# Gate products of a product-key expert layer: one 128-column matmul per token and half in place of two of 64 columns

## The chip, the cores and the metric

The kernel runs on one core of a Trainium2 chip. The metric is device time in microseconds (us), from the first to the last instruction of the program plus what lies around them, and a lower time is better. A core has five engines with queues of their own: TensorE (PE in the profile; its weight loads are listed apart as PEld), VectorE (DVE), ScalarE (ACT), GpSimd (POOL) and SyncE (SP), which here only starts transfers. Matmul results go to PSUM, eight banks of 512 fp32 values per partition; DVE and ACT read them from there.

## The reference, cut to what matters

The program is two transformer blocks on 256 tokens of width 1024. The change touches one layer of the first block, the expert layer. For each token and each of 8 heads it takes the 16 best of 128 x 128 experts, found as sums of two lists of sub-scores, and a softmax over those 16 gives gates:

```python
    cand_i = (top_i[..., 0, :, None] * PEER_NKEYS + top_i[..., 1, None, :])...
    fin_s, fin_pos = lax.top_k(cand_s, PEER_TOPK)
    expert_idx = jnp.take_along_axis(cand_i, fin_pos, axis=-1)
    gates = jax.nn.softmax(fin_s, axis=-1)
...
        u_sel = jnp.take(u, ec, axis=0)
        act = jax.nn.gelu(jnp.einsum('chkd,cd->chk', u_sel, hc), approximate=False) * gc
        v_sel = jnp.take(v, ec, axis=0)
        return jnp.einsum('chk,chkd->cd', act, v_sel)
```

An expert is a pair (i, j) of indices below 128. So each token has 128 selections (8 heads times 16), each with an i, a j and a gate.

## The kernel before, in words

The kernel gathers nothing. It computes the activations of all 16384 experts for all tokens, multiplies them by a dense gate matrix that is zero where an expert was not selected, and multiplies the result by all of v. Expert (i, j) lies at unit i, partition j.

The U stage has 128 units, one for each i. A unit is one weight tile of 128x1024 fp32 (512 KB). SP loads it (`w`, line 322), ACT rounds it to `wh` (line 288), POOL subtracts to get the rest `wl` (line 292), and PE runs 24 matmuls of 256 columns from line 370: 16 with `wh` (against the high and the low part of the activations) and 8 with `wl`. ACT then writes GELU of the bank into `Ah` (line 1234). `Ah[0]` holds units 0 to 63, `Ah[1]` units 64 to 127. There are three buffers each of `w`, `wh` and `wl`. The V stage has 128 units too: for each, ACT and DVE split one unit of `Ah` into `zz` (lines 241 and 238), and PE runs 24 matmuls into four PSUM banks that accumulate over the whole stage (lines 1341, 1343 and 1345).

Between the two stand the gates. For a token, the gate matrix of one half (64 values of i) is a product over its 128 selections: a one-hot of j (128 selections x 128 j) as the stationary operand, and a one-hot of i times the gate (128 selections x 64 i) as the moving one. The gate is kept as two fp16 parts, `sel[0]` and `sel[1]`, so that there are two products per token, which add up in PSUM. `gbatch` does 8 tokens: DVE builds the j one-hot `ohJ` (line 1251), the i one-hot `ohI` (line 1253) and its two products with the gate parts `gI` (line 1256), all in fp16 and all with the token as the innermost index; PE runs 16 matmuls (line 1264) into one bank; and DVE multiplies the bank into `Ah` in place (line 1268). A half has 32 batches, in two lanes that alternate (`gate_lane`). Half 0 runs beside units 64 to 127 of the U stage, half 1 beside the first units of the V stage; unit 64 of the V stage needs all of half 1.

The order on each engine comes from a planner in the kernel, `Sched`. Work is written as generators of `Op`s with an engine, a cost in ns and dependencies. The planner keeps a clock per engine, emits the op that can start first by these costs, and places PE's main work with `sch.pe`, which first lets everything be emitted that could start before it. An op for PE is held back by `SLACK` (450 ns). A higher cost on DVE therefore moves the ops behind it, and the gate matmuls that depend on them, to a later place among PE's units. Each engine then runs its queue strictly in that order.

Of the kernel before, what the change touches and what calls it, by code (L numbers as in the profile page):

```python
# [24 lines left out]
AF = mybir.ActivationFunctionType  # L25
OP = mybir.AluOpType
# [4 lines left out]
S = 256  # L31
# [169 lines left out]
def tile_kernel(ctx, tc, A, out):  # L201
    nc = tc.nc
    V, ACT, POOL, PE, SP = nc.vector, nc.scalar, nc.gpsimd, nc.tensor, nc.sync
# [684 lines left out]
    for i, (key, j) in enumerate(order2):  # L888
# [7 lines left out]
        g = post_gate(key, j) if key in ("gs", "gc") else posts[key](j)  # L896
# [146 lines left out]
    acc2 = cpool.tile([128, S], F32, name="accp")  # L1043
    RpD = cpool.tile([128, 384], F32, name="RpD")
# [15 lines left out]
    hT = cpool.tile([128, 2, S], F32, name="hT")  # L1060
# [157 lines left out]
    sm_ = epool.tile([128, 16 * S], HF, tag="e0b", name="selT")  # L1218
    for i, key in enumerate(("i", "j", 0, 1)):
        sel[key] = sm_[:, i * S:(i + 1) * S]  # L1220
    iotax = sm_[:, 5 * S:9 * S].rearrange("p (n t) -> p n t", t=8)

    def prep_iota():
        yield Op("dve", c_dve(1024), lambda: V.tensor_copy(iotax, iota[:, :, None].to_broadcast([128, 128, 8])),
                 ev="iotax")

    sch.spawn(prep_iota(), prio=900.0)

    Ah = [None, None]
# [11 lines left out]
    ohF = [None]  # L1241

    def gbatch(hh, t0, pool):
        q = (t0 // 8) % 2
        ohJ = ohF[0][:, q * 1024:(q + 1) * 1024].rearrange("p (n t) -> p n t", t=8)
        ohI = ohF[0][:, 2048:2560].rearrange("p (n t) -> p n t", t=8)
        gb = ohF[0][:, 2560:4096] if q == 0 else sm_[:, 9 * S:15 * S]
        gI = [gb[:, i * 512:(i + 1) * 512].rearrange("p (n t) -> p n t", t=8) for i in range(2)]
        sl = slice(t0, t0 + 8)
        bc = lambda v, n: v[:, None, sl].to_broadcast([128, n, 8])  # L1250
        yield Op("dve", c_dve(1024, 0, True), lambda: V.tensor_tensor(
            ohJ, iotax, bc(sel["j"], 128), op=OP.is_equal), deps=[("sel", t0 // 128), "iotax", ("Gp", hh, t0 - 16)])
# [5 lines left out]
        b = [None]

        def f():  # L1260
            b[0] = pool()
            for t in range(8):
                for i in range(2):
# [566 lines left out]
    for n in range(4):  # L1830
        p = mmb()
# [7 lines left out]
    for s in range(2):  # L1839
        p = mmb()  # L1840
# [270 lines left out]
```

## Time and profile before

| | |
|---|---|
| median of 3 runs | 1807.87 us (1806.69 to 1808.79) |
| the profiled execution | 1811.32 us, its span 1809.5 us |
| busy share of the span | PE 93%, DVE 68%, POOL 66%, ACT 44% |
| granted TensorE clock, mean | 0.954 |
| matmuls | 13460 |

The profile gives for each engine the time its instructions took; an instruction that waits for a shared resource after it has started counts as busy. The chain that ended last is followed back from the last instruction, at each step to what released it. A granted clock of 1 is 2.4 GHz, and half of it 1.2 GHz. A row that merges several instructions says how many there were behind an x.

### The profile page before, as it was taken

Reading aid. Unit: us, or ns where it says so; the run is one execution under the profiler, and the core shown is the slowest. Engines: PE = TensorE matmul, PEld = TensorE weight load, DVE = VectorE, ACT = ScalarE, POOL = GpSimd, SP = SyncE. Lnnn points to the kernel's source line nnn. Section 1 sums busy time; section 2 is a strip of 40 time slices with the busy share of each in tenths; the row PEclk is TensorE's granted clock in tenths of the full one; section 3 lists DMA queues with packets and bytes.
Section 4 is the critical chain, followed back from the end, with each engine's and each line's share of the span. In section 5 each row is a group of like instructions: output and inputs, shape, how many; then the busy total and the mean of one; then the engine's idle time right before and its main releaser. Section 6 shows DMA issues by size and latency. Waiting matters only on the chain.

```text
span 1809.5 us, 33154 instructions
## 1 busy us (share of the span) xinstructions
PE 1688.5 (93%) x13460; PEld 1666.1 (92%) x13460; DVE 1222.8 (68%) x1994; ACT 803.3 (44%) x1302; POOL 1185.9 (66%) x509
## 2 busy tenths in 40 slices
PE   8898989898996999999999999999999889979997
PEld 7898989898996999999999999999999878979997
DVE  7999966658998706776006777889787897474302
ACT  5533445555443442222443223444444545656533
POOL 5677865456685884444884556887688633768885
PEclk8999999999998998888999999999999999999999
DMA  6454644445453453222553334555455331545553
GB/s 200 151 175 146 192 163 141 129 129 165 148 182 115 150 179 115 94 94 94 171 180 117 115 117 129 186 180 161 152 186 181 120 102 65 165 139 176 185 187 117
DMA packets 75305, 266.73 MB, mean 147 GB/s; under 512 B 8720, under 2 KB 9232, under 8 KB 75152
## 3 DMA queue, kind: packets, MB, share of 16 engines
q1 hardware_dynamic: 73856, 262.77, 44.8%
q8 instruction: 105, 1.72, 0.4%
q10 hardware_dynamic: 1296, 1.85, 0.3%
q14 instruction: 48, 0.39, 0.1%
HBM read 262.48 MB, written 2.10 MB: 146 GB/s over the span
## 4 chain that ended last, share of the span: by engine, by line
PE 61%; DVE 33%; ACT 3%; issue 2%; DMA 1%; POOL 0%; SPq 0%; DVEq 0%; ACTq 0%; POOLq 0%
PE mmb L370 29%; PE msb L1343 7%; PE msb L1341 7%; PE msb L1345 7%; DVE msb L607 5%; PE msb L1264 4%; PE mmb L1264 4%; DVE zz L238 3%; DVE scr L1182 1%; DVE scy L662 1%; DVE scr L1143 1%; DVE scr L1140 1%; ACT wh L288 1%; DVE scr L1179 1%; DVE scr L1142 1%
## 5 line engine op out<-in xcount | busy, mean ns | idle before, releaser
L292 POOL TENSOR_TENSOR wl<-w,wh 128x1024 fp32r<-128x1024 f32 x473 | 1162.2, 2461 | 591.4 <-ACT wh L288 413.3
L288 ACT ACTIVATE wh<-w 128x1024 fp32r<-128x1024 f32 x491 | 518.4, 1059 | 587.9 <-PE msb L1343 260.1
L238 DVE TENSOR_TENSOR zz<-Ah,zz 128x256 fp32r<-128x256 f32 x128 | 216.4, 1693 | 140.0 <-ACT zz L241 140.0
L370 PE MATMUL mmb<-hA,wh 128*128 128x256 f32 x1024 | 263.8, 293 | 1.2 <-ACT wh L288 1.2
L370 PE MATMUL mmb<-hB,wh 128*128 128x256 f32 x1024 | 262.1, 291 | 0.0
L1343 PE MATMUL msb<-zz,wh 128*128 128x256 f32 x1008 | 252.1, 287 | 7.8 <-DVE zz L238 7.7
L1341 PE MATMUL msb<-zz,wh 128*128 128x256 f32 x1008 | 253.2, 288 | 0.8 <-ACT zz L241 0.8
L370 PEld LDWEIGHTS mmb<-hA,wh 128*128 128x128 f32 x1024 | 206.6, 202 | 1.4 <-ACT wh L288 1.4
L370 PEld LDWEIGHTS mmb<-hB,wh 128*128 128x128 f32 x1024 | 205.6, 201 | 0.0
L1343 PEld LDWEIGHTS msb<-zz,wh 128*128 128x128 f32 x1008 | 197.1, 196 | 8.8 <-DVE zz L238 8.8
L1341 PEld LDWEIGHTS msb<-zz,wh 128*128 128x128 f32 x1008 | 197.2, 196 | 1.0 <-ACT zz L241 1.0
L370 PE MATMUL mmb<-hA,wl 128*128 128x256 f32 x1024 | 156.3, 299 | 0.4 <-POOL wl L292 0.4
L1345 PE MATMUL msb<-zz,wl 128*128 128x256 f32 x1008 | 145.0, 287 | 0.0
L370 PEld LDWEIGHTS mmb<-hA,wl 128*128 128x128 f32 x1024 | 142.1, 205 | 0.6 <-POOL wl L292 0.6
L370 PE MATMUL mmb<-hN,wh 128*128 128x256 f32 x896 | 120.4, 286 | 13.3 <-ACT hN L241 5.5
L1345 PEld LDWEIGHTS msb<-zz,wl 128*128 128x128 f32 x1008 | 132.3, 195 | 0.0
L1264 PEld LDWEIGHTS <-ohF 128*128 128x128 f16 x1024 | 121.5, 146 | 11.2 <-DVE ohF L1256 6.0
L370 PEld LDWEIGHTS mmb<-hN,wh 128*128 128x128 f32 x896 | 113.2, 195 | 15.3 <-ACT wh L288 6.7
L607 DVE SCALAR_TENSOR_TENSOR msb<-glu,vec,msb 128x256 f32<-128x256 f32 x232 | 113.1, 487 | 6.2
L1268 DVE SCALAR_TENSOR_TENSOR Ah<-msb,Ah 128x512 f32<-128x512 f32 x32 | 22.1, 692 | 101.3 <-PE msb L1264 101.3
L1234 ACT ACTIVATE Ah<-mmb 128x256 f32<-128x256 f32 x128 | 47.1, 368 | 84.0 <-PE mmb L370 84.0
L370 PE MATMUL mmb<-eu,wh 128*128 128x256 f32 x512 | 70.7, 287 | 6.4 <-DVE uHL L474 2.7
(465 smaller groups left out, 3268.1 us busy)
## 6 DMA issues: line engine op xcount, KB each, us to landing
w<-in_peer_u_dram SPq DMA_DIRECT2D x128, 512.0 KB, 3.5
w<-in_peer_v_dram SPq DMA_DIRECT2D x128, 512.0 KB, 3.5
w<-in_w_in_dram SPq DMA_DIRECT2D x81, 512.0 KB, 3.5
w<-in_w_up_dram SPq DMA_DIRECT2D x32, 512.0 KB, 3.5
w<-in_w_down_dram SPq DMA_DIRECT2D x32, 512.0 KB, 3.5
w<-in_w_peer_q_dram SPq DMA_DIRECT2D x16, 512.0 KB, 3.7
w<-in_w_v_dram SPq DMA_DIRECT2D x8, 512.0 KB, 3.5
w<-in_sc_w_out_dram SPq DMA_DIRECT2D x8, 512.0 KB, 3.6
```

The lines of the kernel that those rows point to most:

```text
L238: return lambda e="dve": ENG[e].tensor_tensor(o, a, b, op=op)
L288: yield Op("act", c_act(1024), lambda: ACT.activation(h, w, AF.Copy), deps=u["wdep"], ev=("H", u["i"]))
L292: lambda e: ENG[e].tensor_tensor(l, w, h.bitcast(F32), op=OP.subtract), ev=("L", u["i"]))
L370: PE.matmul(p[:, :S], a, b, start=first and n == 0, stop=last and n == len(todo) - 1)
L607: lambda k=k: V.scalar_tensor_tensor(cc[:, j] if k == 30 else o(), glu[:, j, k:k + S], vcol("cf_w", j * 31 + k), o(), op0=OP.mult, op1=OP. ...
L662: lambda k=k: V.scalar_tensor_tensor(y, b[:, k:k + S], vcol("sc_w", j * 3 + k), y, op0=OP.mult, op1=OP.add),
L1234: yield Op("act", c_act(S), lambda: ACT.activation(Ah[n // 64][:, n % 64], p[:, :S], AF.Gelu), ev=("U", n))
L1264: PE.matmul(b[0][:, t * 64:(t + 1) * 64], ohJ[:, :, t], gI[i][:, :, t], start=i == 0, stop=i == 1)
L1268: yield Op("dve", c_dve(512), lambda: V.scalar_tensor_tensor(z, b[0].rearrange("p (t i) -> p i t", t=8), 1.0 / GS, z, op0=OP.mult, op1=OP. ...
L1341: PE.matmul(o, u["H"][:, d, :], opH, start=first and d % 2 == 0, stop=False, skip_group_check=True)
L1343: PE.matmul(o, u["H"][:, d, :], opL, start=False, stop=False, skip_group_check=True)
L1345: PE.matmul(o, u["L"][:, d, :], opH, start=False, stop=last, skip_group_check=True)
```

## The change

`gbatch` is rewritten. The j one-hot stays as it was, with its token innermost. The i one-hot is built in token order (`p t n`) from a contiguous row `iotan` of the numbers 0 to 127, which ACT copies once as fp16. One DVE instruction of 1024 elements multiplies it by both gate parts, which lie side by side in `sel["g"]`, into `gT` (token, part, i). A token then needs one matmul whose moving operand is 128 contiguous columns, 64 for each part, and eight tokens fill two banks in two ops of four matmuls. The parts no longer add up in the accumulation: ACT copies the low half of a bank into fp32 scratch, DVE adds it to the high half in the bank, and DVE multiplies that into `Ah`. The scratch is `hT`, `RpD` and `accp`, which are free there. The planner's costs of the three DVE ops are written as 1000, 900 and 1700 ns, a gate matmul is put at 85 ns in place of 30, and the last ops have events of their own. The pool of banks is as before: `msb` in half 0, `mmb` in half 1, four banks each.

```diff
+    sel["g"] = sm_[:, 2 * S:4 * S].rearrange("p (a s) -> p a s", a=2)
+    iotan = sm_[:, 12 * S:12 * S + 128]
+    G_J, G_I, G_T = 1000.0, 900.0, 1700.0
...
-        yield Op("dve", c_dve(1024, 0, True), lambda: V.tensor_tensor(
-            ohJ, iotax, bc(sel["j"], 128), op=OP.is_equal), deps=[("sel", t0 // 128), "iotax", ("Gp", hh, t0 - 16)])
-        yield Op("dve", c_dve(512, 0, True), lambda: V.tensor_tensor(
-            ohI, iotax[:, hh * 64:(hh + 1) * 64], bc(sel["i"], 64), op=OP.is_equal), deps=[("Gi", hh, t0 - 8)])
-        for i in range(2):
-            yield Op("dve", c_dve(512, 0, True), lambda i=i: V.tensor_tensor(
-                gI[i], ohI, bc(sel[i], 64), op=OP.mult), ev=("Gi", hh, t0) if i == 1 else None)
...
-                    PE.matmul(b[0][:, t * 64:(t + 1) * 64], ohJ[:, :, t], gI[i][:, :, t], start=i == 0, stop=i == 1)
...
-        yield Op("pe", 16 * 30.0, f, ev=("Gp", hh, t0))
-        z = Ah[hh][:, :, sl]
-        yield Op("dve", c_dve(512), lambda: V.scalar_tensor_tensor(
-            z, b[0].rearrange("p (t i) -> p i t", t=8), 1.0 / GS, z, op0=OP.mult, op1=OP.mult), ev=("Z", hh, t0))
+        yield Op("dve", G_J, lambda: V.tensor_tensor(
+            ohJ, iotax, sel["j"][:, None, sl].to_broadcast([128, 128, 8]), op=OP.is_equal),
+            deps=[("sel", t0 // 128), "iotax", ("Gp", hh, t0 - 16)])
+        yield Op("dve", G_I, lambda: V.tensor_tensor(
+            ohI, iotan[:, None, hh * 64:(hh + 1) * 64].to_broadcast([128, 8, 64]),
+            sel["i"][:, sl][:, :, None].to_broadcast([128, 8, 64]), op=OP.is_equal), deps=[("Gi", hh, t0 - 8)])
+        yield Op("dve", G_T, lambda: V.tensor_tensor(
+            gT, ohI[:, :, None].to_broadcast([128, 8, 2, 64]),
+            sel["g"][:, :, sl].rearrange("p a t -> p t a")[:, :, :, None].to_broadcast([128, 8, 2, 64]),
+            op=OP.mult), ev=("Gi", hh, t0))
...
+                    PE.matmul(banks[c][:, t * 128:(t + 1) * 128], ohJ[:, :, 4 * c + t], gT[:, 4 * c + t],
+                              start=True, stop=True, skip_group_check=True)
...
+            yield Op("pe", 4 * 85.0, f(c), chain=c == 0, ev=("Gp", hh, t0) if c else ("Gc", hh, t0))
...
+            yield Op("act", 380.0, lambda view=view, lc=lc: ACT.activation(lc, view(1), AF.Copy),
+                     deps=[("Gp", hh, t0) if c else ("Gc", hh, t0)], chain=False, ev=("Ga", hh, t0, c))
+            yield Op("dve", c_psum(256), lambda view=view, lc=lc: V.tensor_tensor(view(0), view(0), lc, op=OP.add),
+                     deps=[("Ga", hh, t0, c)], chain=False, ev=("Gs", hh, t0, c))
+            yield Op("dve", c_psum(256), lambda view=view, z=z: V.scalar_tensor_tensor(
+                z, view(0), 1.0 / GS, z, op0=OP.mult, op1=OP.mult), deps=[("Gs", hh, t0, c)], chain=False,
+                ev=("Z", hh, t0) if c else None)
```

Lines behind the change are shifted: the gate matmuls stand at line 1274 of the changed kernel (1264 before), the three DVE ops at 1255, 1259 and 1262, the copy at 1284, the sum at 1286 and the multiplication at 1288.

On PE the order before in half 0 is 32 gate matmuls (both lanes), then 48 matmuls of U units, and so on 16 times, with 776 U matmuls behind the last. The changed order settles into 8 gate matmuls, 40 U matmuls, 8 gate matmuls and 56 U matmuls. Its first gate matmul stands 24 U matmuls later than before (576 behind the last transpose of the selection, where it was 552), and its last one 32 U matmuls ahead of the end of the stage. In half 1 the order before has 16 gate matmuls on either side of 8 V matmuls, once in every two units, and ends at unit 32. The changed order has 8 gate matmuls about every two units, from the third unit on, and its last three batches (24 matmuls) stand together behind unit 63.

DVE's queue in half 0 of the kernel before, one pair of batches (`ohF` and `selT` hold the one-hots, `msb` is the bank):

```order
L1251 TENSOR_TENSOR ohF<-selT 128x1024 x2
L1253 TENSOR_TENSOR ohF<-selT 128x512
L1256 TENSOR_TENSOR ohF<-ohF,selT 128x512 x2
L1253 TENSOR_TENSOR ohF<-selT 128x512
L1256 TENSOR_TENSOR selT<-ohF,selT 128x512 x2
L1268 SCALAR_TENSOR_TENSOR Ah_5368<-msb,Ah_5368 128x64x8 x2
```

And DVE's queue at the same place of the changed kernel, one batch and a half:

```order
740 L1255 TENSOR_TENSOR ohF_7689<-selT_5367 128x1024
741 L1259 TENSOR_TENSOR ohF_7689<-selT_5367 128x512
742 L1286 TENSOR_TENSOR msb_7916<-msb_7916,hT_4607 128x64x4
743 L1262 TENSOR_TENSOR selT_5367<-ohF_7689,selT_5367 128x1024
744 L1288 SCALAR_TENSOR_TENSOR Ah0_5368<-msb_7916,Ah0_5368 128x64x4
745 L1286 TENSOR_TENSOR msb_7921<-msb_7921,hT_4607 128x64x4
746 L1288 SCALAR_TENSOR_TENSOR Ah0_5368<-msb_7921,Ah0_5368 128x64x4
```

Before, both lanes' one-hots stand ahead of the two ops that wait for PE. Now the sum of the other lane (which waits for PE and then ACT) stands ahead of the product `gT` on which the next gate matmuls depend, and a batch has seven DVE instructions in place of five.

DVE's queue in half 1 of the kernel before, where `zz` is the split of `Ah` for the V units:

```order
895 L1251 TENSOR_TENSOR ohF_7688<-selT_5367 128x1024
896 L1256 TENSOR_TENSOR ohF_7688<-ohF_7688,selT_5367 128x512
897 L238 TENSOR_TENSOR zz_10442<-Ah0_5368,zz_10442 128x256
898 L1256 TENSOR_TENSOR ohF_7688<-ohF_7688,selT_5367 128x512
899 L1253 TENSOR_TENSOR ohF_7688<-selT_5367 128x512
900 L1256 TENSOR_TENSOR selT_5367<-ohF_7688,selT_5367 128x512 x2
901 L1268 SCALAR_TENSOR_TENSOR Ah1_7687<-mmb_11056,Ah1_7687 128x64x8
```

And in half 1 of the changed kernel:

```order
983 L1286 TENSOR_TENSOR mmb_10672<-mmb_10672,RpD_4281 128x64x4
984 L1262 TENSOR_TENSOR ohF_7689<-ohF_7689,selT_5367 128x1024
985 L238 TENSOR_TENSOR zz_10347<-Ah0_5368,zz_10347 128x256
986 L1288 SCALAR_TENSOR_TENSOR Ah1_7688<-mmb_10672,Ah1_7688 128x64x4
987 L1286 TENSOR_TENSOR mmb_10677<-mmb_10677,accp_4280 128x64x4
988 L1288 SCALAR_TENSOR_TENSOR Ah1_7688<-mmb_10677,Ah1_7688 128x64x4
989 L1255 TENSOR_TENSOR ohF_7689<-selT_5367 128x1024
990 L238 TENSOR_TENSOR zz_10347<-Ah0_5368,zz_10347 128x256
991 L1286 TENSOR_TENSOR mmb_10756<-mmb_10756,hT_4607 128x64x4
992 L1259 TENSOR_TENSOR ohF_7689<-selT_5367 128x512
```

The `zz` splits, which the next V units wait for, now stand between the new sums, each of which waits for PE and ACT.

## Rows read from the trace of the kernel before

**Rows 1.** The page: busy time by engine, and its chain by line.
```profile
PE 1688.5 (93%) x13460; PEld 1666.1 (92%) x13460; DVE 1222.8 (68%) x1994; ACT 803.3 (44%) x1302; POOL 1185.9 (66%) x509
...
PE mmb L370 29%; PE msb L1343 7%; PE msb L1341 7%; PE msb L1345 7%; DVE msb L607 5%; PE msb L1264 4%; PE mmb L1264 4%; DVE zz L238 3%; DVE scr L1182 1%; DVE scy L662 1%; DVE scr L1143 1%; DVE scr L1140 1%; ACT wh L288 1%; DVE scr L1179 1%; DVE scr L1142 1%
```

**Rows 2.** The chain in half 0: start, duration (us), what.
```profile
616.55 68.29 PE mmb L370 x552
684.84 3.95 PE msb L1264 x32
688.79 7.23 PE mmb L370 x48
696.01 3.95 PE msb L1264 x32
```

**Rows 3.** The chain from the end of the U stage into half 1.
```profile
857.20 94.50 PE mmb L370 x776
...
952.00 0.42 ACT zz L241
...
966.78 0.21 PE msb L1341
...
970.56 0.12 PE msb L1341
...
972.48 1.97 PE mmb L1264 x16
```

**Rows 4.** Windows: length, busy PE, PEld, DVE, ACT, POOL, clock, DMA share, GB/s.
```profile
684.00:858.00 174.00, 168.71 (x1244) 166.91 (x1244) 129.33 (x152) 42.76 (x61) 78.95 (x31) 0.85 0.30 98
...
960.00:1113.00 153.00, 152.61 (x1241) 151.01 (x1240) 113.48 (x186) 43.27 (x61) 77.91 (x31) 0.98 0.35 114
```

**Rows 5.** Timeline of PE: five fp32 matmuls of 128 columns, and what follows.
```profile
443.05 0.77 PE L1129 MATMUL msb<-pqF 128*128 128x128 f32 x5 [0.43 <-DVE pqF L474]
443.66 0.33 PE L370 MATMUL mmb<-pe0a,wh 128*128 128x256 f32 x1
```

**Rows 6.** Instructions of line 1264: ns min/median/max, first and last start.
```profile
L1264 PE MATMUL mmb<-selT,ohF x256: 295/302/333, 964.1 to 1112.9; 128*128 128x64 f16 x128
```

**Rows 7.** DVE and ACT instructions by line, ns min/median/max, first and last start.
```profile
L1251 DVE TENSOR_TENSOR ohF<-selT x30: 678/682/686, 963.2 to 1104.8; 128x1024 f16<-128x1024 f16 x30
...
L238 DVE TENSOR_TENSOR zz<-Ah,zz x31: 411/416/482, 959.8 to 1105.8; 128x256 fp32r<-128x256 f32 x31
...
L1268 DVE SCALAR_TENSOR_TENSOR Ah<-mmb,Ah x31: 690/691/693, 962.6 to 1110.3; 128x512 f32<-128x512 f32 x31
...
L1179 DVE TENSOR_TENSOR scr<-scr,cst x8: 1216/2175/3446, 556.6 to 609.1; 128x1024 f32<-128x1024 f32 x8
...
L238 DVE TENSOR_TENSOR mmb<-mmb,R x44: 416/432/433, 22.9 to 1707.4; 128x256 f32<-128x256 f32 x44
...
L1234 ACT ACTIVATE Ah<-mmb x128: 361/365/387, 474.0 to 951.7; 128x256 f32<-128x256 f32 x128
```

**Rows 8.** POOL's `wl` without gates beside it, and DVE's `zz` beside POOL.
```profile
L292 POOL TENSOR_TENSOR wl<-w,wh x32: 2377/2400/2400, 859.1 to 949.1; 128x1024 fp32r<-128x1024 f32 x32
...
L292 POOL TENSOR_TENSOR wl<-w,wh x43: 2397/2405/2600, 1116.3 to 1237.3; 128x1024 fp32r<-128x1024 f32 x43
...
L238 DVE TENSOR_TENSOR zz<-Ah,zz x40: 2417/2428/2433, 1116.6 to 1228.9; 128x256 fp32r<-128x256 f32 x40
```

**Rows 9.** Timeline of DVE and of POOL, where both always have work.
```profile
564.57 2.18 DVE L1179 TENSOR_TENSOR scr<-scr,cst 128x1024 f32<-128x1024 f32 x1
566.79 3.25 DVE L1182 TENSOR_TENSOR scr<-scr 128x1024 f32<-128x1024 f32 x1
570.07 1.22 DVE L1185 TENSOR_REDUCE scr<-scr 128x64 f32<-128x1024 f32 x1
571.21 2.12 DVE L1179 TENSOR_TENSOR scr<-scr,cst 128x1024 f32<-128x1024 f32 x1
...
562.56 12.96 POOL L292 TENSOR_TENSOR wl<-w,wh 128x1024 fp32r<-128x1024 f32 x4 [0.24 <-ACT wh L288]
```

More of the change, by code (lines that the diff above doesn't have):

```diff
@@ L1220, in tile_kernel @@
         sel[key] = sm_[:, i * S:(i + 1) * S]
-    iotax = sm_[:, 5 * S:9 * S].rearrange("p (n t) -> p n t", t=8)
+    sel["g"] = sm_[:, 2 * S:4 * S].rearrange("p (a s) -> p a s", a=2)
+    iotax = sm_[:, 4 * S:8 * S].rearrange("p (n t) -> p n t", t=8)
+    iotan = sm_[:, 12 * S:12 * S + 128]
+    G_J, G_I, G_T = 1000.0, 900.0, 1700.0
     def prep_iota():
+        yield Op("act", c_act(128), lambda: ACT.activation(iotan, iota, AF.Copy))
         yield Op("dve", c_dve(1024), lambda: V.tensor_copy(iotax, iota[:, :, None].to_broadcast([128, 128, 8])),
@@ L1245, in gbatch @@
         ohJ = ohF[0][:, q * 1024:(q + 1) * 1024].rearrange("p (n t) -> p n t", t=8)
-        ohI = ohF[0][:, 2048:2560].rearrange("p (n t) -> p n t", t=8)
-        gb = ohF[0][:, 2560:4096] if q == 0 else sm_[:, 9 * S:15 * S]
-        gI = [gb[:, i * 512:(i + 1) * 512].rearrange("p (n t) -> p n t", t=8) for i in range(2)]
+        ohI = ohF[0][:, 2048:2560].rearrange("p (t n) -> p t n", t=8)
+        gT = ohF[0][:, 2560:3584] if q == 0 else sm_[:, 8 * S:12 * S]
+        gT = gT.rearrange("p (t a n) -> p t a n", t=8, a=2)
@@ L1249, in gbatch @@
         sl = slice(t0, t0 + 8)
-        bc = lambda v, n: v[:, None, sl].to_broadcast([128, n, 8])
-        yield Op("dve", c_dve(1024, 0, True), lambda: V.tensor_tensor(
-            ohJ, iotax, bc(sel["j"], 128), op=OP.is_equal), deps=[("sel", t0 // 128), "iotax", ("Gp", hh, t0 - 16)])
-        yield Op("dve", c_dve(512, 0, True), lambda: V.tensor_tensor(
-            ohI, iotax[:, hh * 64:(hh + 1) * 64], bc(sel["i"], 64), op=OP.is_equal), deps=[("Gi", hh, t0 - 8)])
-        for i in range(2):
-            yield Op("dve", c_dve(512, 0, True), lambda i=i: V.tensor_tensor(
-                gI[i], ohI, bc(sel[i], 64), op=OP.mult), ev=("Gi", hh, t0) if i == 1 else None)
@@ L1258, in gbatch @@
[L1258 to L1263, printed above, removed]
-                    PE.matmul(b[0][:, t * 64:(t + 1) * 64], ohJ[:, :, t], gI[i][:, :, t], start=i == 0, stop=i == 1)
-        yield Op("pe", 16 * 30.0, f, ev=("Gp", hh, t0))
-        z = Ah[hh][:, :, sl]
-        yield Op("dve", c_dve(512), lambda: V.scalar_tensor_tensor(
-            z, b[0].rearrange("p (t i) -> p i t", t=8), 1.0 / GS, z, op0=OP.mult, op1=OP.mult), ev=("Z", hh, t0))
+        yield Op("dve", G_J, lambda: V.tensor_tensor(
+            ohJ, iotax, sel["j"][:, None, sl].to_broadcast([128, 128, 8]), op=OP.is_equal),
+            deps=[("sel", t0 // 128), "iotax", ("Gp", hh, t0 - 16)])
@@ new lines, in gbatch, with f, g @@
+        lo = ((hT[:, 0], hT[:, 1]), (RpD[:, :S], acc2[:, :]))[q]
+        banks = [None, None]
+        def f(c):
+            def g():
+                banks[c] = pool()
+                for t in range(4):
+                    PE.matmul(banks[c][:, t * 128:(t + 1) * 128], ohJ[:, :, 4 * c + t], gT[:, 4 * c + t],
+                              start=True, stop=True, skip_group_check=True)
+            return g
+        for c in range(2):
+            yield Op("pe", 4 * 85.0, f(c), chain=c == 0, ev=("Gp", hh, t0) if c else ("Gc", hh, t0))
@@ new lines, in gbatch @@
+        for c in range(2):
+            view = lambda i, c=c: banks[c].rearrange("p (t a i) -> p a i t", t=4, a=2)[:, i]
+            lc = lo[c].rearrange("p (i t) -> p i t", t=4)
+            z = Ah[hh][:, :, t0 + 4 * c:t0 + 4 * c + 4]
+            yield Op("act", 380.0, lambda view=view, lc=lc: ACT.activation(lc, view(1), AF.Copy),
[5 more added lines that the diff above has]
+                ev=("Z", hh, t0) if c else None)
```

## The prediction

> **What bounds the kernel now.** I read the page first. PE is busy for 93% of the span, and of the chain that ended last most is matmuls; the gate matmuls of line 1264 have two entries of 4% each [rows 1]. So in most of the program PE sets the pace, and time taken from PE there is time taken from the end, unless another engine comes up to it.
>
> Next the chain in the two stretches that the change touches. I call A the time from 616.55, where half 0's stretch begins, to the first `zz` of the V stage at 952.00 [rows 2, 3]: 335.5 us. In A the chain is all PE: 552 U matmuls in 68.29 us, then in turn 32 gate matmuls in 3.95 us and 48 U matmuls in 7.23 us, and at the end 776 U matmuls in 94.50 us [rows 2, 3]. A U matmul takes 94.50/776 = 0.122 us at the end. Between gate blocks it takes 7.23/48 = 0.151 us. The windows say why: the granted clock is 0.85 in the gate stretch of half 0, and 0.98 in that of half 1 [rows 4]. After 32 gate matmuls in a row PE runs for some microseconds at the lower level of 1.2 GHz; one sees such a spell in half 1 too, after a wait, where matmuls start 0.21 us apart and later 0.12 us, while 16 gate matmuls in 1.97 us are not followed by one [rows 3]. So half 0 loses 7.23 - 48 x 0.122 = 1.4 us per pair of batches, over 15 gaps 21 us.
>
> B is the time from 952.00 to the start of V unit 64, which needs all of half 1. The last gate matmul starts at 1112.9 [rows 6], and 32 units follow at the pace of POOL's 43 starts, (1237.3 - 1116.3)/42 = 2.881 us [rows 8]. B is 160.9 + 92.2 = 253.1 us.
>
> Then who else is near its limit there. POOL needs 2.40 us per unit of 2.88 us [rows 8]. DVE's two-input instructions wait for POOL: `zz` takes 0.416 us where POOL is off and 2.428 us where POOL always runs [rows 7, 8], the difference being most of a POOL instruction. So POOL's `wl` and every DVE instruction that reads two operands from SBUF share something that one of them holds at a time; I call it the port. DVE instructions with an operand in PSUM don't wait: 690 to 693 ns, always [rows 7].
>
> **The change part by part.** *Gate matmuls, removed.* 1024 become 512. What does one of 128 columns cost? Before, one of 64 fp16 columns takes 3.95/32 = 0.123 us [rows 2]. Five fp32 matmuls of 128 columns take 443.66 - 443.05 = 0.61 us, 0.122 each [rows 5], and U's of 256 columns the same 0.122. The pace doesn't follow the columns up to 256; the stationary side, unchanged here, sets it. Lower bound for the new one 0.061, half of it (no row here is faster than 0.12, but the moving operand is contiguous now); upper bound 0.245 (twice the columns, twice the time). I take 0.122, the nearest row. That is 256 x 0.122 = 31.2 us per half in place of 63.
>
> The Trainium skill (TensorE: Matmul & The Clock Gate, section Back-to-back issue gap) gives about 81 ns for a sustained stream with 128 columns. The row shows 122 ns. By the page a half would have 20.7 us of them, 10 less; in the sum below PE's pace is not the bound, so that it would not move.
>
> *The slow clock, removed.* Blocks are of 8 now, half of those of 16 that left the clock at 0.98 [rows 4]. I count U matmuls at 0.122.
>
> *DVE's one-hots, changed.* The j one-hot stays at 0.682 us [rows 7]. The i one-hot (512 elements) and the product (1024) have an operand repeated along the innermost index. The trace has no fp16 row of that kind. Lower bound: they keep the pace of line 1251, 0.682 us per 1024 and 0.42 per 512. Upper bound: the fp32 instruction of line 1179, the same shape with the same kind of repeated operand, 1.216 us unhindered [rows 7]; with `zz`'s 0.416 for 256 the slope is 0.800/768 = 1.04 ns per element, and 512 cost 0.683. I take the upper bound, since line 1179 is the row with that operand. Port time per batch is then 0.682 + 0.683 + 1.216 = 2.58 us.
>
> The Trainium skill (VectorE: DVE Perf Modes, What auto-detection actually checks) says that two results per cycle need 16-bit tensors with a step of 1 or -1, in every tensor. A repeated operand has a step of 0. The page speaks against this change, and agrees with the row that I took. By the lower bound 0.79 us per batch would go, and the forecast below would be about 40 us lower.
>
> *ACT's copies, DVE's sums, added.* 128 copies at about 0.37 us (line 1234 [rows 7]) are 47 us of ACT, which is busy 43 of 174 and 43 of 153 us there [rows 4]; hidden, at most 0.37 us of delay for a `wh` behind each. On DVE four PSUM instructions of 256 elements, 0.43 us each (line 238 on the bank [rows 7]), take the place of one of 0.69: 1.72 us per batch. They need no port, and can run while POOL does. If that cover goes, 1.72 x 64 = 110 us in place of 44 lie open.
>
> *Now the sum of the port.* In A the gates lie beside 2048 - 576 = 1472 U matmuls, 61.3 units, and 30 of the 32 batches are built there (two lanes are filled ahead, as before). POOL 61.3 x 2.40 = 147.2; DVE 30 x 2.58 = 77.4; together 224.6 us. PE: 1472 x 0.122 + 31.2 = 210.5 (by 94.50/776 unrounded). So the port overtakes PE. In B: POOL 64 x 2.405 = 153.9, `zz` 64 x 0.416 = 26.6, gates 32 x 2.58 = 82.6, together 263.1; PE 64 x 2.881 + 31.2 = 215.6.
>
> Lower bound of the port: some of an instruction doesn't hold it. From 564.57 to 571.21 pass 6.64 us [rows 9], with two DVE port instructions of 1.22 and, since POOL has one running whenever DVE waits, two of POOL's 2.40. (6.64 - 4.80)/2 = 0.92: each DVE instruction hides 0.30. A batch then costs 1.69, `zz` 0.12, and the sums are 198 in A and 215.7 in B, at PE's pace or below. Against that, both queues are strict: when DVE's head is a sum that waits for PE, nobody uses the port. I take the full sums, as if the hidden 0.30 paid for these gaps.
>
> A becomes 576 x 68.29/552 = 71.3 ahead of the gates, plus 224.6: 295.9, **39.6 less**. B becomes 263.1, plus the tail: three batches stand together ahead of unit 64, and behind the last one only its own chain runs (8 matmuls 0.98, copy 0.37, four DVE steps 1.72, `zz` 0.40 and 0.42): 3.9 us. 267.0, **13.9 more**. In sum 25.7 us less: the profiled execution at 1811.3 - 25.7 = 1785.6, and the median, 3.45 lower, at 1782.
>
> **Rivals.** *PE keeps the pace.* The lower port sums hold, and DVE and POOL fit beside PE: A 71.3 + 210.5 (-53.7), B 215.7 + 3.9 (-33.5), together -87: 1721. For it: in half 1 before, 32 batches at 1.95 us (one of 0.68, three of 0.42), 32 `zz` and 32 of POOL are 153 us of port in a window of 153, and PE was busy throughout [rows 4], so a full port need not hurt. Against it: that PE had more of its own then. The keeping of DVE's faster pace leads near it, to about 1743.
>
> *Slower: DVE's queue in half 1 never hides POOL.* Each POOL instruction finds DVE at a port instruction, as `zz` does all along rows 8, and the PSUM steps run only when POOL is off. A batch with two units then costs 2.58 + 1.72 + 0.83 + 4.81 = 9.94 us, B 318 + 3.9 = 322 (+69), and with A's -39.6 the kernel is 29 slower: 1837. It decides from 9.03 us per batch on, (253.1 + 39.6 - 3.9)/32; the forecast has 8.22. For it: the product stands behind the other lane's sum, and `zz` between them, so that a wait for PE passes on to PE. Against: POOL starts behind ACT's `wh`, not behind DVE, so that some overlap is likely.
>
> *The products cost by the column*, 0.245 each: PE 242 in A, -22, B still by the port, +14: 1800. Against it are rows 5.
>
> **How the numbers follow.** Forecast 0.52, PE's pace 0.20, slower 0.21, columns 0.07. The forecast's own range is 1762 to 1806. For 8 in 10 I take half of either outer case: 1738 to 1820. A measurement here tells 0.2%, 3.6 us, from no change. Faster: 0.48 of the forecast, 0.19 and 0.05, in sum 0.72. Same: 0.08. Slower: 0.20.
>
> **What would show it.** Right: gate matmuls 0.12 us apart, a clock near 0.95 or above in half 0, the product near 1.2 us unhindered, POOL's `wl` at more than 2.5 us on average beside the gates, PE waiting there for `wl` and for the product, A near 296 and B near 267. Wrong: PE without gaps in both halves (then 1721), B above 290 with DVE busy throughout (then slower), gate matmuls at 0.2 us or more.

## The result, and the profile after

The changed kernel takes 1783.82 us (median), the kernel before 1808.33 us beside it: ratio 0.9862, 95% interval 0.9838 to 0.9885. One of the four executions after was slow (1920.76 us, with a granted clock of 0.742); it is in the median and not in the ratio. The forecast was 1782. The profiled execution after is 1783.02 us, with a span of 1781.2.

I cut both spans at the same places: up to the last transpose of the selection, from there to the first `zz` (A), from there to V unit 64 (B), and the rest. So measured, the span before is 615.9 + 336.1 + 253.2 + 604.3, and after 613.3 + 286.8 + 272.2 + 608.8. A lost 49.3 us (forecast 39.6), B gained 19.0 (forecast 13.9), the rest gained 4.5, and the unchanged start lost 2.5. Unchanged code alone moves by amounts like the last two: over the runs below the start varies from 608 to 616, and the rest from 599 to 609.

First the page after: busy time by engine, and its chain by line. It answers to [rows 1].

```profile
PE 1605.8 (90%) x12948; PEld 1579.4 (89%) x12948; DVE 1362.3 (76%) x2122; ACT 839.0 (47%) x1431; POOL 1210.3 (68%) x509
...
PE mmb L370 7%; DVE zz L238 5%; PE msb L1362 5%; PE msb L1364 5%; PE msb L1366 5%; DVE ohF L1259 2%; DVE selT L1262 2%; DVE ohF L1262 1%; DVE ohF L1255 1%; DVE mmb L1286 1%; DVE Ah L1288 1%; DVE prT L1681 1%; DVE angS L1402 1%; DVE aS L238 0%; ACT wh L288 0%
```

PE has 83 us less to do and DVE 140 more. The gate matmuls have left the chain, and the one-hots and the product (lines 1255, 1259, 1262) are on it in their place.

The windows after: length, busy PE, PEld, DVE, ACT, POOL, clock, DMA share, GB/s. The first is the gate stretch of half 0, the next two half 1, and then what follows it.

```profile
684.00:900.00 216.00, 199.63 (x1732) 195.84 (x1730) 207.27 (x218) 100.86 (x187) 164.12 (x62) 0.99 0.44 152
912.00:1040.00 128.00, 109.26 (x878) 107.20 (x877) 124.99 (x136) 52.62 (x95) 82.96 (x32) 0.92 0.39 134
1040.00:1170.00 130.00, 103.99 (x850) 101.29 (x848) 124.55 (x140) 49.59 (x89) 80.13 (x31) 0.91 0.37 129
1170.00:1195.00 25.00, 22.78 (x172) 22.46 (x171) 17.51 (x14) 11.11 (x19) 14.43 (x6) 0.86 0.32 110
1195.00:1300.00 105.00, 98.56 (x778) 98.16 (x777) 90.55 (x73) 46.24 (x69) 77.87 (x33) 0.93 0.48 162
```

Beside [rows 4] the two halves have changed places. Half 0 has its clock back (0.99, before 0.85), and PE is busy for 92% of it. In half 1 DVE is busy for 96 to 98% of the time, PE for 80 to 85%, and the clock has fallen to 0.91.

PE's waits in half 0 (684 to 900), and then in half 1 (905 to 1176): us in total, times, longest.

```profile
PE msb L1274 <- DVE ohF L1262: 12.2, 13, 1.1
PE msb L1274 <- DVE selT L1262: 4.0, 1, 4.0
```
```profile
PE mmb L1274 <- DVE selT L1262: 34.4, 13, 4.9
PE mmb L1274 <- DVE ohF L1262: 12.7, 6, 2.8
```

PE waits for the product in both halves, 16 us in the one and 47 in the other. What the low clock looks like behind such a wait stands in PE's timeline of half 0:

```profile
694.05 0.70 PE L1274 MATMUL msb<-ohF 128*128 128x128 f16 x8
694.55 1.20 PE L370 MATMUL mmb<-hA,wl 128*128 128x256 f32 x8
...
702.61 1.07 PE L1274 MATMUL msb<-selT,ohF 128*128 128x128 f16 x8 [3.98 <-DVE selT L1262]
703.44 0.56 PE L370 MATMUL mmb<-hA,wh 128*128 128x256 f32 x1
703.80 0.42 PE L370 MATMUL mmb<-hB,wh 128*128 128x256 f32 x1
704.01 0.41 PE L370 MATMUL mmb<-hA,wh 128*128 128x256 f32 x1
```

Eight products and no wait: the next matmul starts 0.50 us later. After the wait of 3.98 us the U matmuls start 0.21 us apart, which is the lower level, 1.2 GHz.

DVE's instructions by line after: ns min/median/max, first and last start.

```profile
L1255 DVE TENSOR_TENSOR ohF<-selT x64: 674/764/2864, 614.9 to 1165.6; 128x1024 f16<-128x1024 f16 x64
...
L1259 DVE TENSOR_TENSOR ohF<-selT x64: 675/682/2891, 616.1 to 1166.6; 128x512 f16<-128x512 f16 x64
...
L1262 DVE TENSOR_TENSOR ohF<-ohF,selT x32: 1207/3157/3402, 619.0 to 1163.7; 128x1024 f16<-128x1024 f16 x32
L1262 DVE TENSOR_TENSOR selT<-ohF,selT x32: 1207/1226/3394, 623.1 to 1167.8; 128x1024 f16<-128x1024 f16 x32
...
L1286 DVE TENSOR_TENSOR mmb<-mmb,hT x32: 415/420/433, 914.1 to 1167.5; 128x256 f32<-128x256 f32 x32
```

The smallest of each is its price unhindered: 0.674, 0.675, 1.207 and 0.415 us. The larger ones hold a POOL instruction. POOL in turn waits for DVE; its `wl` in half 0 (684 to 900) and in half 1 (912 to 1160): busy us, mean ns, against the 2400 of [rows 8].

```profile
L292 POOL TENSOR_TENSOR wl<-w,wh 128x1024 fp32r<-128x1024 f32 x62 | 165.3, 2666 | 51.7 <-ACT wh L288 51.3 <-DMA w<-in_peer_u_dram 0.3
```
```profile
L292 POOL TENSOR_TENSOR wl<-w,wh 128x1024 fp32r<-128x1024 f32 x62 | 163.1, 2635 | 86.2 <-ACT wh L288 61.6 <-PE msb L1366 23.3 <-PE mmb L1274 1.3
```

Last the end of half 1 on PE, from the low matmuls of V unit 63 to unit 64:

```profile
1155.19 1.19 PE L1366 MATMUL msb<-zz,wl 128*128 128x256 f32 x8
1161.31 1.07 PE L1274 MATMUL mmb<-selT,ohF 128*128 128x128 f16 x8 [4.93 <-DVE selT L1262]
1164.96 1.08 PE L1274 MATMUL mmb<-ohF 128*128 128x128 f16 x8 [2.57 <-DVE ohF L1262]
1169.08 1.07 PE L1274 MATMUL mmb<-selT,ohF 128*128 128x128 f16 x8 [3.05 <-DVE selT L1262]
1172.37 0.58 PE L1362 MATMUL msb<-zz,wh 128*128 128x256 f32 x1 [2.22 <-ACT zz L241]
```

Three batches are built one after the other while PE has nothing else. Of B's 272.2 us, 256.0 are up to unit 63 (I call it the body) and 16.3 are this tail.

### The profile page after: what moved, and what is told of

Same layout as the page of the kernel before. It is cut to its first block, busy times and chain, and to the rows that moved or that the text cites. A ratio compares the mean times of both kernels' runs of the same rounds, so it can differ in the third digit from the quotient of the medians.

```text
span 1781.2 us, 32465 instructions
## 1 busy us (share of the span) xinstructions
PE 1605.8 (90%) x12948; PEld 1579.4 (89%) x12948; DVE 1362.3 (76%) x2122; ACT 839.0 (47%) x1431; POOL 1210.3 (68%) x509
## 5 line engine op out<-in xcount | busy, mean ns | idle before, releaser
L292 POOL TENSOR_TENSOR wl<-w,wh 128x1024 fp32r<-128x1024 f32 x473 | 1186.6, 2514 | 539.8 <-ACT wh L288 437.5
L1364 PE MATMUL msb<-zz,wh 128*128 128x256 f32 x1008 | 260.0, 293 | 6.9 <-DVE zz L238 6.8
L1362 PE MATMUL msb<-zz,wh 128*128 128x256 f32 x1008 | 260.8, 293 | 3.0 <-ACT zz L241 3.0
L370 PE MATMUL mmb<-hB,wh 128*128 128x256 f32 x1024 | 254.9, 286 | 0.0
L1364 PEld LDWEIGHTS msb<-zz,wh 128*128 128x128 f32 x1008 | 203.6, 202 | 8.1 <-DVE zz L238 8.1
L1362 PEld LDWEIGHTS msb<-zz,wh 128*128 128x128 f32 x1008 | 203.6, 202 | 3.4 <-ACT zz L241 3.4
L370 PE MATMUL mmb<-hA,wl 128*128 128x256 f32 x1024 | 146.3, 286 | 0.0
L370 PEld LDWEIGHTS mmb<-hA,wl 128*128 128x128 f32 x1024 | 133.2, 193 | 0.0
L1274 PEld LDWEIGHTS <-ohF 128*128 128x128 f16 x512 | 38.7, 151 | 71.3 <-DVE selT L1262 41.3
L1259 DVE TENSOR_TENSOR ohF<-selT 128x512 f16<-128x512 f16 x64 | 98.9, 1545 | 0.0
L1255 DVE TENSOR_TENSOR ohF<-selT 128x1024 f16<-128x1024 f16 x64 | 80.9, 1265 | 0.0
L1262 DVE TENSOR_TENSOR ohF<-ohF,selT 128x1024 f16<-128x1024 f16 x32 | 79.1, 2473 | 0.1
```

What stands on the lines that cost most here:

```text
L292: lambda e: ENG[e].tensor_tensor(l, w, h.bitcast(F32), op=OP.subtract), ev=("L", u["i"]))
L370: PE.matmul(p[:, :S], a, b, start=first and n == 0, stop=last and n == len(todo) - 1)
L1255: yield Op("dve", G_J, lambda: V.tensor_tensor(ohJ, iotax, sel["j"][:, None, sl].to_broadcast([128, 128, 8]), op=OP.is_equal), deps=[("sel ...
L1259: yield Op("dve", G_I, lambda: V.tensor_tensor(ohI, iotan[:, None, hh * 64:(hh + 1) * 64].to_broadcast([128, 8, 64]), sel["i"][:, sl][:, : ...
L1262: yield Op("dve", G_T, lambda: V.tensor_tensor(gT, ohI[:, :, None].to_broadcast([128, 8, 2, 64]), sel["g"][:, :, sl].rearrange("p a t -> p ...
L1274: PE.matmul(banks[c][:, t * 128:(t + 1) * 128], ohJ[:, :, 4 * c + t], gT[:, 4 * c + t], start=True, stop=True, skip_group_check=True)
```

## The experiments

All of them in one table, in us. Times are medians, ratios are to the kernel before in the same runs; A and B are read from the one profiled execution of each kernel, and a difference of them is one of single executions. B is split into the body, up to the end of V unit 63, and the tail. "Port" is the full sum for half 1 as the prediction made it (POOL's 153.9, `zz`'s 26.6, and 32 batches with that kernel's own unhindered durations).

| run | time | ratio (95%) | A | B = body + tail | port in B |
|---|---|---|---|---|---|
| before | 1808 | | 336.1 | 253.1 + 0.1 | 243 |
| after | 1783.8 | 0.9862 (0.9838 to 0.9885) | 286.8 | 256.0 + 16.3 | 263 |
| e1_half0_only | 1758.3 | 0.9756 (0.9710 to 0.9803) | 286.8 | 253.0 + 0.1 | 243 |
| e2_two_of_64 | 1798.2 | 0.9963 (0.9937 to 0.9989) | 297.8 | 259.6 + 15.1 | 263 |
| e3_token_inner | 1787.6 | 0.9894 (0.9863 to 0.9925) | 308.6 | 243.7 + 13.1 | 237 |
| e4_old_costs | 1828.2 | 1.0143 (1.0091 to 1.0195) | 318.4 | 293.6 + 0.1 | 263 |
| e5_two_products_no_sums | 1775.5 | 0.9813 (0.9797 to 0.9829) | 297.8 | 260.3 + 0.5 | 263 |
| e6_token_pairs | 1797.3 | 0.9934 (0.9918 to 0.9951) | 284.5 | 275.7 + 14.2 | 249 |
| e7_pairs_two_products | 1770.8 | 0.9782 (0.9753 to 0.9812) | 292.7 | 259.6 + 0.1 | 249 |
| e8_short_rest | 1726.2 | one run | 286.6 | 202.4 + 15.3 | 138 |
| e9_before_spread | 1802.5 | 0.9968 (0.9954 to 0.9981) | 309.7 | 255.9 + 10.5 | 243 |
| e10_half1_pairs | 1742.9 | 0.9637 (0.9614 to 0.9660) | 287.8 | 240.9 + 0.1 | 243 |

**The change in half 0 alone.** Half 1 keeps the old batch.

```diff
-            yield from gbatch(hh, t0, pool)
+            yield from (gbatch_old if hh else gbatch)(hh, t0, pool)
```

> Half 0 as changed, half 1 with the gate batch of before (two products of 64 columns, four fast DVE one-hots, no sums). Theory: the change gains in A (it measured 284 us against 335.5 before) and loses in B (272 against 253) and a few us behind B by the low clock; undoing half 1 keeps A at 284 and brings B back to 253, so 1756 to 1764 us. Rival, the planner's order or the clock makes the difference in both halves together: B stays above 265 and the time within 8 us of the changed kernel's 1784.

A is the same as with the whole change, and B the same as before. So the change is two changes: a gain in half 0 and a loss in half 1, and without the loss the kernel is at 1758, 25 us better.

**Two products of 64 columns, still contiguous.**

```diff
-                    PE.matmul(banks[c][:, t * 128:(t + 1) * 128], ohJ[:, :, 4 * c + t], gT[:, 4 * c + t],
+                    for a in range(2):
+                        PE.matmul(banks[c][:, t * 128 + a * 64:t * 128 + a * 64 + 64], ohJ[:, :, 4 * c + t],
+                                  gT[:, 4 * c + t, a],
```

> The changed kernel with two products of 64 contiguous columns per token in place of one of 128, into the same bank columns; everything else and the order as changed. Theory (half the products is what A gains from): 256 more products a half at 0.122 us, A rises by about 31 us to 312 to 318, B, where DVE is late, by 0 to 15, the time 1812 to 1828 us. Rival (A gains from the new order and the clock, not from the count): A rises by less than 10, the time 1784 to 1795 us.

PE's timeline of half 0 in this kernel:

```profile
692.62 1.17 PE L1275 MATMUL msb<-ohF 128*128 128x64 f16 x16
693.62 1.20 PE L370 MATMUL mmb<-hA,wl 128*128 128x256 f32 x8
```

Sixteen in 1.00 us: 0.063 each, half of the 0.123 in [rows 2], with the same stationary side. So the theory's 0.122 per product was wrong, and A rose by 11.0 us, between the 31 of the theory and the less than 10 of the rival. Per half these products are 32 us. By the same measure, from the first start to the start of what follows, the eight of 128 columns take 0.50 us in the rows of half 0 above and 0.52 in most blocks, 16 to 17 us per half. Of the 15 us or so between them, 11.0 come out in A and 2.5 in B.

**The changed kernel with the token innermost again**, in the one-hot of i and in the product; instructions, planner's costs and sums as changed.

```diff
-        gT = gT.rearrange("p (t a n) -> p t a n", t=8, a=2)
+        gT = gT.rearrange("p (a n t) -> p a n t", t=8, a=2)
...
-                    PE.matmul(banks[c][:, t * 128:(t + 1) * 128], ohJ[:, :, 4 * c + t], gT[:, 4 * c + t],
+                    PE.matmul(banks[c][:, t * 128:(t + 1) * 128], ohJ[:, :, 4 * c + t], gT[:, :, :, 4 * c + t],
```

> The changed kernel with the token innermost in the i one-hot and in its product with the gate parts, so that no operand is repeated along the innermost index; the moving operand of the 128 columns is then strided by 8 elements. Costs and order as changed. Theory (the repeated operand halves DVE's pace, and the stationary side sets the pace of a product): the product takes 0.68 us unhindered and the i one-hot 0.42, products stay 0.12 us apart, B falls from 272 by about 25 to 245 to 252, A by 0 to 3, the time 1750 to 1764 us. Rival 1 (contiguous columns are what lets 128 cost 0.12): products 0.18 to 0.25 us apart, A rises by 15 to 30, the time 1785 to 1810. Rival 2 (B is late because of POOL and the strict queues, whatever the pace): B above 265, the time 1775 to 1785.

PE's timeline in half 0, and then two of DVE's lines:

```profile
695.24 2.07 PE L1274 MATMUL msb<-ohF 128*128 128x128 f16 x8
696.94 1.32 PE L370 MATMUL mmb<-hA,wl 128*128 128x256 f32 x8
```
```profile
L1259 DVE TENSOR_TENSOR ohF<-selT x64: 406/415/2654, 616.9 to 1171.7; 128x512 f16<-128x512 f16 x64
L1262 DVE TENSOR_TENSOR ohF<-ohF,selT x32: 673/692/2575, 617.4 to 1169.0; 128x1024 f16<-128x1024 f16 x32
```

This is the trade that the change makes. With a step of 16 bytes in the moving operand a product of 128 columns takes 1.70/8 = 0.2125 us by that measure; DVE is back at 0.41 and 0.67 us. A is 21.8 us worse than with the change, B 15.4 better.

**The planner's old costs with the new code.**

```diff
-    G_J, G_I, G_T = 1000.0, 900.0, 1700.0
+    G_J, G_I, G_T = 600.0, 333.0, 600.0
```

> The changed kernel with the planner's costs of the three DVE one-hot ops put back to the formula of before (600, 333 and 600 ns); the work is the same, the gates stand closer together on PE, ends 26 units ahead of the U stage's end and 14 units earlier in half 1. Theory (DVE and the port set the pace of the gates whatever the plan): PE waits for the product at most of the gate blocks, the low clock shows in half 0 too, and what is lost beside the gates is partly won behind them: 1775 to 1800 us. Rival (the written costs are what the change gains from): 1805 us or more.

Slower than before, by 1.4%. PE's waits in half 1 (905 to 1176):

```profile
PE mmb L1274 <- DVE selT L1262: 56.6, 16, 4.0
```

By the old numbers the batches of half 1 stand in twos, 72 V matmuls apart, and nearly each such block waits for its product. The clock is 0.84 there (930 to 1150), and 0.90 in half 0 while its gates run (676 to 850). The even placement is worth 1828.2 - 1783.8 = 44 us.

**The spread alone, on the kernel before.**

```diff
-        yield Op("dve", c_dve(1024, 0, True), lambda: V.tensor_tensor(
+        yield Op("dve", 1200.0, lambda: V.tensor_tensor(
...
-            yield Op("dve", c_dve(512, 0, True), lambda i=i: V.tensor_tensor(
+            yield Op("dve", 900.0, lambda i=i: V.tensor_tensor(
```

> The kernel before with nothing changed but the planner's costs of its DVE ops (1200, 900, 900, 900 and 1100 ns), so that its gate blocks are of 16, spread over the U stage to within 6 units of its end and over 64 units of half 1, about as in the changed kernel. Theory (the spread takes the low clock out of half 0): A falls from 336 to 308 to 318, B 250 to 262, time 1780 to 1800 us, so that the written costs are worth about as much as the new products. Rival (the count and the layout of the products make the gain): A above 328, time 1800 to 1812.

The window of half 0:

```profile
684.00:900.00 216.00, 216.00 (x1788) 214.50 (x1787) 130.06 (x149) 74.20 (x108) 137.92 (x55) 1.00 0.41 135
```

In blocks of 16 with U matmuls between, the clock is 1.00 and PE has no gap: A falls by 26.4. Half 1 gives half of it back, since spreading its batches over all 64 units leaves a tail of 10.5.

**Without the sums**: two products per token add up in the bank as before, so that the copies on ACT and the sums on DVE go. The one-hots are as changed, but the planner's costs are raised (1300, 1200 and 2100), and with them the order is another one: no batch stands behind V unit 63.

```diff
-                              start=True, stop=True, skip_group_check=True)
+                    PE.matmul(b[0][:, t * 64:(t + 1) * 64], ohJ[:, :, t], gT[:, t, a], start=a == 0, stop=a == 1)
```

> The changed one-hots in token order, but two products of 64 contiguous columns that add up in the bank, and one multiplication per batch, as before: no copies on ACT, no sums on DVE. One-hot costs raised (1300, 1200, 2100 ns) so that the gates stay spread (one batch per 1.7 units in half 0, 1.9 in half 1). From the last runs: contiguous products of 64 stand 0.063 us apart, those of 128 0.081 us, strided ones 0.123 and 0.21. Theory P (half 1 is late by POOL and the slow one-hots, 2.58 us per batch, at one shared port): A 285 to 295, B 262 to 275, time 1770 to 1790 us. Theory Q (half 1 is late by the sums, 1.03 us more of DVE per batch, and the way over ACT): B 245 to 256, time 1752 to 1768.

A is as in the run with two products and sums (297.8), so that there is no sign that the sums cost anything in half 0. In half 1 B is 14 us better than there, nearly all of it the tail. The order changed together with the sums, and no run here separates the two. (The 0.081 us in the expectation is not what the rows show; there eight products of 128 columns take 0.50 to 0.52 us.)

**Pairs of tokens** innermost, one product of 128 columns and the sums (the first), or two products and no sums (the second). The product with the gate is two instructions of 512 in both. The first splits the planner's cost of it among them, the second has costs of its own and with them an order of its own.

```diff
-        gT = gT.rearrange("p (t a n) -> p t a n", t=8, a=2)
+        gT = gT.rearrange("p (u a n w) -> p u a n w", u=4, a=2, w=2)
```

> The changed kernel with pairs of tokens innermost in the i one-hot and its products with the gate parts (two instructions of 512), so that no operand is repeated innermost and the moving columns have a step of 2 elements, 4 bytes; one product of 128 and the sums as changed, gates spread as changed. Theory: DVE's fast pace comes back (0.42 us per 512 unhindered) and a step of 4 bytes costs PE nothing (0.08 us a product): A 283 to 290, B 252 to 262 as with the token innermost (258.8), time 1758 to 1772 us. Rival 1, any step costs as a step of 8 does: products 0.21 us apart, A 300 or more, 1780 to 1795. Rival 2, runs of two are not enough for the fast pace: 0.68 us per 512, B 272 or more, 1785 or more.

> Token pairs innermost, and two products of 64 columns with a step of 2 that add up in the bank, one multiplication per batch, no sums; gates spread (one batch per 1.5 units in half 0, 1.7 in half 1). DVE does per batch what it did before, PE half of the time per product. Theory (PE's strided reading, DVE's slow one-hots and the order are what there is to win): A 283 to 290, B 225 to 245, time 1735 to 1755 us, faster than either kernel. Rival (the spread alone sets it and half 1 cannot go below the 253 of before): B 250 to 260, time 1755 to 1770.

The products with the gate get DVE's fast pace back, 0.403 us for 512 at the least, but the one-hot of i takes 0.60: its row of numbers lay in pairs 16 bytes apart. The first has the best A of all and a body of B 27 us over its port sum. There DVE was idle for ACT (930 to 1150):

```profile
DVE mmb L1288 <- ACT accp L1286: 13.8, 5, 3.0
DVE zz L238 <- ACT zz L241: 10.4, 5, 2.2
DVE mmb L1288 <- ACT hT L1286: 8.1, 5, 1.9
```

These are 32 us in that window, against 6 in the changed kernel; 21.9 of them are the sums (line 1288), which wait for the copies. The second, without sums, has a body of 259.6, but it too waits for ACT's `zz`, 19.7 us in the same window. So a part of the hop over ACT is likely and not shown, and why it costs so much in this order and not in that of the change stays open.

**POOL's share of the port taken away in half 1.**

```diff
-                 lambda e: ENG[e].tensor_tensor(l, w, h.bitcast(F32), op=OP.subtract), ev=("L", u["i"]))
+                 lambda e: ENG[e].tensor_tensor(l[:, r], w[:, r], h[:, r].bitcast(F32), op=OP.subtract),
+                 ev=("L", u["i"]))
```

> The changed kernel, but for the V units 0 to 63 POOL subtracts only one of the eight slices of 128 columns, and the eight low matmuls of such a unit all read that slice: most of the low part of these units is left out. Order and number of instructions are those of the changed kernel; a POOL instruction of that kind should take about 0.3 to 0.4 us in place of 2.40. Theory (the port makes half 1 late: POOL's subtraction keeps DVE's two-operand instructions waiting): B falls from 274 to PE's own pace with small waits, 205 plus a tail of 5 to 15, so 210 to 225; the product and the one-hots take 1.21 and 0.68 us on average, and the granted clock there is 0.97 or more. Rival (the order of DVE's queue: the sums wait for PE and ACT, and the product behind them): B stays above 250, with PE waiting for the product (line 1262) as before. A, untouched, 284 to 290.

The body of B falls from 256.0 to 202.4 us; the clock is 1.00 from 912 to 1040. POOL's instruction takes 0.46 us at the median, and nearly every product on DVE (line 1264 here) its unhindered time:

```profile
L1264 DVE TENSOR_TENSOR ohF<-ohF,selT x16: 1207/1215/1227, 903.8 to 1108.8; 128x1024 f16<-128x1024 f16 x16
```

The chain of waits from 902 to 922 has only PE:

```profile
902.83 0.96 PE msb L1368 x8
...
905.71 0.96 PE msb L1368 x8
...
908.59 0.54 PE mmb L1276 x8
909.13 1.01 PE msb L1368 x8
...
912.06 0.56 PE mmb L1276 x8
912.61 1.01 PE msb L1368 x8
...
915.54 0.96 PE msb L1368 x8
...
921.89 0.96 PE msb L1368 x8
```

A unit is 2.88 us (905.71 - 902.83). The six from 902.83 to 921.89 take 19.06 with three blocks of products among them, so that a block of 8 costs (19.06 - 17.28)/3 = 0.593 us, 0.074 per product. (This is more than the 0.063 to 0.065 from start to start: a part of the cost shows only behind the block.) And 64 x 2.88 + 29 x 0.593 = 201.5 is the body. The other 53.6 us of the changed kernel's body stood there because DVE and POOL shared the port. PE's and DVE's order in half 1 and the number of instructions were the same, so the order of DVE's queue by itself is not the cause.

**Half 0 as changed, half 1 in pairs of tokens**, in the old order, from a row of numbers that holds each of them twice.

```diff
+    iotap = sm_[:, 14 * S:15 * S].rearrange("p (n w) -> p n w", w=2)
...
-        gI = [gb[:, i * 512:(i + 1) * 512].rearrange("p (n t) -> p n t", t=8) for i in range(2)]
+        gI = [gb[:, i * 512:(i + 1) * 512].rearrange("p (u n w) -> p u n w", u=4, w=2) for i in range(2)]
```

> Half 0 as in the changed kernel, half 1 with the instructions and the order of the kernel before (two products of 64 columns per token, no sums), but the one-hot of i and its two products with the gate are stored for pairs of tokens (i, then the two tokens innermost), from a row that holds each number twice. The moving operand then has a step of 4 bytes in place of 16. Expected: gate matmuls of half 1 0.063 us apart in place of 0.123, so PE has 512 x 0.06 = 31 us less to do. Theory (PE bounds half 1 of the kernel before): B falls from 253 to 222 to 232, the kernel to about 1732. Rival (the port is full there too: per batch 1.95 of DVE, 0.42 of the split and 2.40 of POOL are 4.77 us, against 4.85 of PE's 2.88 + 1.97): B stays at 248 to 253, PE waits for the one-hots and the splits, and the kernel is within 0.3% of the 1758 of the kernel that changes half 0 alone. If an instruction with runs of two loses DVE's fast pace (0.60 in place of 0.42), the port needs 5.3 us per batch, and B is about 270.

The best version: 1742.9 us, 3.6% less than before. One of its one-hots, and its chain over a pair of batches:

```profile
L1306 DVE TENSOR_TENSOR ohF<-selT x32: 409/424/2600, 905.8 to 1047.3; 128x512 f16<-128x512 f16 x32
```
```profile
911.12 1.03 PE msb L1398 x8
912.15 1.03 PE mmb L1317 x16
...
913.20 0.69 DVE Ah L1321
913.89 1.11 DVE zz L238
...
916.61 2.54 DVE ohF L1309
...
919.20 1.05 PE mmb L1317 x15
920.25 1.03 PE msb L1398 x8
```

The products are 0.063 apart, and DVE keeps its pace. But B went down by 12 us and not by the 31 that PE was spared, to between the 222 to 232 of the theory and the 248 to 253 of the rival. (Beside the profiled execution with half 0 alone, the unchanged code moved too: the start is 6 us longer and the rest 5 shorter.) A round of two units takes 9.13 us, and the port's sum for it is 2 x (1.93 + 0.42 + 2.40) = 9.5. B ends within 2 us of the port's 243. That is close, but not a proof that the port alone bounds it: the chain of a round has 3.1 us of PE, 0.69 of a multiplication on PSUM that needs no port, and only one wait for a whole POOL instruction (the 2.54), where POOL runs two. It is a loop from DVE over PE and back, with the port's wait in it.

## Why the prediction was right, point by point

*A gate product costs 0.122, since the stationary side sets the pace.* The number is wrong, and the reason at least incomplete. The stationary one-hot has a step of 16 bytes in every kernel here, and the price moves with the step of the moving operand: from start to start, 64 columns cost 0.123 with a step of 16 bytes and 0.063 with one of 2 or 4; 128 columns 0.2125 with 16 bytes and 0.063 to 0.065 with 2. So at 16 bytes the price does follow the columns, as in my last rival, and with adjacent columns it does not. What sets the 0.063 no run here shows. I took the pace of products with a step of 16 bytes for one without. A product cost 0.074 in effect, 19.0 us per half and not 31.2. The Trainium skill's 81 ns (TensorE: Matmul & The Clock Gate, Back-to-back issue gap), which I set aside for my row, was nearer to the 74.

*"PE's pace is not the bound, so that it would not move."* This is the step that failed in half 0. With products at the price that I forecast (two of 0.063) A is 297.8, within 2 us of the forecast 295.9; with the real ones it is 286.8. Of the 15 us or so taken from PE, 11 came out, though DVE was busy for 96% of the stretch. PE's own sum is 71.3 + 1472 x 94.5/776 + 19.0 = 269.6, and its waits for the product add 16.2; so A is 17 above PE's sum and 9 below the port's. The full sum of the port is thus no floor either, and where the 9 us are hidden stays open. With the two sums this close, no single one of them gave the time.

*The slow clock goes.* Right: 0.99. But blocks of 8 are not needed for it, nor are they enough: the old blocks of 16 give 1.00 once U matmuls stand between them, and blocks of 8 with waits (the old costs) give 0.90. It is the planner's placement. By the spread alone A falls by 26.4 us, more than half of its 49.3.

*DVE's prices.* Right within some 2%: 0.675 where 0.683 was forecast, 1.207 for 1.216, the sums 0.42 for 0.43. DVE lost its fast pace by the repeated operand (0.406 and 0.673 without it, token innermost), as the Trainium skill's rule has it (VectorE: DVE Perf Modes, What auto-detection actually checks).

*ACT's copies hidden, the sums run beside POOL.* Nothing in half 0 speaks against it (the same A without them, in another order). In half 1 the run without them has no tail, but no batch behind unit 63 either, so that their part in the tail is not shown.

*The port in half 1.* Right, and shown by taking POOL's part away (PE's waits are for the product alone, though; I had named `wl` too). 263.1 was forecast for all of B. The port time of the last two batches, 5.2 us, and of a third one's one-hot of i and product, 1.9, falls into the tail; that leaves 256.0 for the body, where 256.0 was measured, closer than such a sum deserves (one POOL instruction at an edge is 2.4). As a rule for the time it does not hold: four runs have the port sum of 263, and their bodies go from 256 to 294 with the order.

*The tail, 3.9 us.* Mis-sized: 16.3. I let only the last batch's chain run there, but three batches stand behind unit 63, and each is built in turn. Behind it the clock is 0.86 for 25 us, where it was 1.00 before. That is not the rest's +4.5, though: from the first matmul of unit 64 to the low ones of unit 125 pass 192.6 us, and 192.3 before. The rest's loss comes later, in code that the change does not touch, and its cause stays open.

*The planner's costs.* I took the order as given and priced it by rows; with the old costs the same code loses 1.4%. So the slower rival hung on three numbers in the planner; its mechanism, DVE's queue never beside POOL, would have put B at 322, and even there B is 294.

The errors have opposite signs: A 9.7 better than forecast by its difference, B 5.1 worse, the rest and the start together 2.0 worse. That the sum came within 3 us is in part luck: a gain in A and a loss in B, each forecast too small, made up for each other.

## What to carry to other kernels

Price a matmul by rows with the same step in the moving operand, not only with the same number of columns. When a change moves work from one engine to another, look at each stage's sums for both, and for what they share: before, DVE was busy for 74% of either half [rows 4], but the port had room in half 0 (31 x 2.40 + 30 x 1.95 = 133 of 174 us) and none in half 1 (153 of 153), so that the change belonged in half 0 alone. And when a stage stands within a few per cent of two limits (half 1 before: PE 64 x 2.881 + 32 x 1.97 = 247, port 243), taking 31 us from one of them brings little more than the distance from the measured time to the other: 12 us here, where 253 and 243 are 10 apart.

## What was not expected of the hardware

- A small matmul's pace depends on the step of the moving operand. From start to start, 128 fp16 columns take 0.063 to 0.065 us at a step of 2 bytes and 0.2125 at 16; 64 columns 0.063 at 2 or 4 bytes and 0.123 at 16. The stationary operand had a step of 16 bytes in all of them; what another step would give was not tried.
- DVE's fast pace for fp16 (0.41 us for 512) holds with an operand that repeats a pair of adjacent elements over and over. With one operand in pairs that lie 16 bytes apart it was 0.60, and with one that repeats a single element 0.675.
